# ifftshift of an 8192 x 8192 matrix: which rows each DMA engine takes, and in which steps

## The chip, the core and the metric

The kernel runs on one NeuronCore of a Trainium2 chip (trn2). The time is device microseconds of one execution; of several runs the median is given. No compute engine takes part in the work: the kernel is 256 DMAs from one tensor in the chip's main memory (HBM) to another. A DMA is issued by an instruction on the queue of the SyncE engine (SP) and is carried out by the core's 16 DMA engines, which share it between them.

## The reference

```
def setup_inputs():
    return {"x": np.random.randn(8192, 8192).astype(np.float32)}

def reference(x):
    return np.fft.ifftshift(x)
```

With even sizes the shift swaps the matrix's quadrants: `out[r, c] = x[(r + 4096) % 8192, (c + 4096) % 8192]`. Nothing is computed; 268.4 MB are read and 268.4 MB written. A row is 8192 floats, 32 KB; half a row is 16 KB and a quarter of a row, the piece that one packet carries, is 8 KB.

## The kernel before

`C` is the row length, `hr` and `hc` are half the rows and half the columns. The loop at lines 40 to 42 goes down the matrix in blocks of `rows` = 16 x `apart` = 64 output rows. For each block, two DMAs are issued on `nc.sync`, by the helper `both` (line 25, the DMA itself at line 27): the first with `col` 0, the second with `col` = `piece` = 2048, a quarter of the columns. The access pattern of each has three levels: 64 rows, then two pieces half a row apart, then 2048 contiguous elements. So the first DMA of a block carries the first and third quarter of 64 rows, the second DMA the second and fourth. On the input side the rows are shifted by `hr` and the two pieces come in opposite order (step `-hc`), which is the swap of the halves.

Each DMA is 64 x 2 pieces of 8 KB, 1 MB. By the names in the code (`ENGINES`, `apart`) the outermost level of 64 rows is cut into sixteen runs of four, so that engine `e` takes rows `4e` to `4e + 3` of the block: neighbouring engines are four rows, 128 KB, apart. An engine's eight packets in one DMA are row by row, in each row the two pieces 16 KB apart.

The order of the work is the order of issue on SP's queue: the program is a plain list of 256 DMAs, and there is no wait in the source. The framework gives the DMAs eight completion counters in turn, and the issue of a DMA waits for the one that used the same counter before, eight places earlier. The lines that the change touches:

```
    apart = 4
    piece = hc // 2
    rows = ENGINES * apart
    for row in range(0, R, rows):
        for col in (0, piece):
            both(nc.sync, row, col, rows, piece)
```

Of the kernel before, what the change touches and what calls it, by code (L numbers as in the profile page):

```python
# [1 line left out]

# [4 lines left out]


ENGINES = 16  # L10


@with_exitstack
def kernel(
    ctx: ExitStack,
    tc: tile.TileContext,
    x: bass.AP,
    out: bass.AP,
):
    nc = tc.nc  # L20
    R, C = x.shape
    hr = R // 2
    hc = C // 2

    def both(queue, row, col, rows, piece):

        queue.dma_start(
            out=bass.AP(out.tensor, out.offset + row * C + col, [[C, rows], [hc, 2], [1, piece]]),
            in_=bass.AP(
                x.tensor,  # L30
                x.offset + (row + hr) % R * C + hc + col,
                [[C, rows], [-hc, 2], [1, piece]],
            ),
        )


    apart = 4
    piece = hc // 2
    rows = ENGINES * apart
    for row in range(0, R, rows):  # L40
        for col in (0, piece):
            both(nc.sync, row, col, rows, piece)


# [1 line left out]
_INS = ['x']  # L46
_OUTS = [((8192, 8192), 'float32')]


def kernel(**inputs):  # L50
    import numpy as _np
    import concourse.bacc as _bacc
    import concourse.tile as _tile
    from concourse import mybir as _mybir
    from concourse.bass_utils import run_bass_kernel_spmd as _run

    nc = _bacc.Bacc("TRN2", target_bir_lowering=False, num_devices=1)  # L57
    arrays, args = {}, []
    for name in _INS:
        a = _np.ascontiguousarray(inputs[name])  # L60
        if a.dtype.kind in "iu":
            a = a.astype(_np.int64)
        arrays[f"in_{name}_dram"] = a
        args.append(nc.dram_tensor(f"in_{name}_dram", a.shape, _mybir.dt.from_np(a.dtype), kind="ExternalInput").ap())
    for i, (shape, dtype) in enumerate(_OUTS):
        dt = _mybir.dt.from_np(_np.dtype(dtype))
        args.append(nc.dram_tensor(f"out_{i}_dram", shape, dt, kind="ExternalOutput").ap())
    with _tile.TileContext(nc) as tc:
        kernel(tc, *args)
    r = _run(nc, [arrays], core_ids=[0])  # L70
    got = tuple(r.results[0][f"out_{i}_dram"] for i in range(len(_OUTS)))
    return got[0]
```

## Time and profile before

| what | value |
|---|---|
| time, median of 3 runs | 811.06 us (810.79 to 811.39) |
| the profiled execution's own time | 810.44 us |
| its span, first to last instruction | 808.7 us |
| DMAs, size, median time from issue to landing | 256, 1,024 KB, 25.1 us |
| packets on the DMA queue | 36,864 |
| busy share of the 16 DMA engines | 99.3% |
| mean rate, one direction | 332 GB/s |
| read and written together | 664 GB/s over the span |

The page of the profile has a row of 40 equal slices of the span: the tenths in which the DMA engines were busy, and the GB/s that they moved in it. The queue's line gives packets, megabytes and the time that the packets took as a share of sixteen engines' span. A packet is one contiguous piece of data (or the small write that counts a completion). "To landing" is from the issuing instruction to the arrival of the last completion. SPq in the list of waits is SP's queue; a wait for a DMA there holds back the next issue. Line numbers are those of the kernel.

### The profile page before, as it was taken

To read this page: it belongs to the slowest core of one execution; us is meant where nothing else is said; L and a number is where in the kernel's file an instruction comes from. 1 tells how busy PE (TensorE), PEld (TensorE's weight loads), DVE (VectorE), ACT (ScalarE), POOL (GpSimd) and SP (SyncE) were. 2 spreads that over 40 slices of the span, in tenths; PEclk is the share of its full clock that TensorE was granted. 3 is DMA by queue.
4 is the path that set the end of the run, shared out by engine and by line. 5 is a ranking of instruction groups with operands and counts; after the bars stand their busy time and mean duration, and the time that the engine had idled before them with its cause. 6 is when DMAs were issued, how large, how long until landed. Compare 5 with 4: busy or idle time off the path is not lost. (4 is left out here: it accounts for less than half of the span.)

```text
span 808.7 us, 301 instructions
## 1 busy us (share of the span) xinstructions
POOL 0.2 (0%) x4
## 2 busy tenths in 40 slices
POOL 0000000000000000000000000000000000000000
DMA  8999999999999999999999999999999999999998
GB/s 301 331 335 329 336 334 330 335 332 336 332 335 334 336 331 334 339 328 335 331 335 339 334 334 337 331 336 330 336 334 331 339 332 334 333 336 331 337 335 294
DMA packets 36866, 268.47 MB, mean 332 GB/s; under 512 B 4096, under 2 KB 4096, under 8 KB 4096
## 3 DMA queue, kind: packets, MB, share of 16 engines
q1 hardware_dynamic: 36864, 268.45, 99.3%
q14 instruction: 2, 0.02, 0.0%
HBM read 268.44 MB, written 268.44 MB: 664 GB/s over the span
## 5 line engine op out<-in xcount | busy, mean ns | idle before, releaser
L57 POOL MEMSET const-bfloat16-1.0<- 128x1 bf16 x1 | 0.1, 102 | 0.0
L57 POOL MEMSET const-uint8-127<- 128x1 uint8 x1 | 0.1, 102 | 0.0
L57 POOL MEMSET const-float32-1.0<- 128x1 f32 x1 | 0.1, 99 | 0.0
L57 POOL MEMSET const-float32-0.0<- 128x1 f32 x1 | 0.1, 98 | 0.2 <-issue 0.2
## 6 DMA issues: line engine op xcount, KB each, us to landing
out_dram<-in_x_dram SPq DMA_DIRECT2D x256, 1024.0 KB, 25.1
```

What stands on the lines that cost most here:

```text
L57: nc = _bacc.Bacc("TRN2", target_bir_lowering=False, num_devices=1)
```

## The change

The helper `both`, whose DMA carries two pieces of each row, becomes `copy`, which takes the access pattern from its caller and carries one piece of each row. A block is now 16 x `per` = 128 rows, and four DMAs are issued for it, for the quarters in the order 1, 3, 2, 4. The pattern's outermost level is now 16 long with a step of one row, the next is 8 long with a step of 16 rows: engine `e` takes rows `e`, `e + 16`, ..., `e + 112` of the block. Neighbouring engines are one row (32 KB) apart, and an engine goes in steps of 16 rows (512 KB). The queue, the size of a piece (8 KB), the size of a DMA (1 MB) and the number of DMAs (64 blocks x 4 = 256) stay.

```diff
-    def both(queue, row, col, rows, piece):
-
+    def copy(queue, row, col, dims):
         queue.dma_start(
-            out=bass.AP(out.tensor, out.offset + row * C + col, [[C, rows], [hc, 2], [1, piece]]),
-            in_=bass.AP(
-                x.tensor,
-                x.offset + (row + hr) % R * C + hc + col,
-                [[C, rows], [-hc, 2], [1, piece]],
-            ),
+            out=bass.AP(out.tensor, out.offset + row * C + col, dims),
+            in_=bass.AP(x.tensor, x.offset + (row + hr) % R * C + (col + hc) % C, dims),
         )
 
 
-    apart = 4
+    per = 8
     piece = hc // 2
-    rows = ENGINES * apart
+    rows = ENGINES * per
     for row in range(0, R, rows):
-        for col in (0, piece):
-            both(nc.sync, row, col, rows, piece)
+        for col in (0, hc, piece, hc + piece):
+            copy(nc.sync, row, col, [[C, ENGINES], [ENGINES * C, per], [1, piece]])
```

## The prediction

> **What bounds the kernel now.** I read the page from its top, then the groups of the issuing line, the waits of the issuing queue, the stages, and last the records of single packets. The page first: the span, the slices, the queues.
>
> ```profile
> span 808.7 us, 301 instructions
> ...
> DMA  8999999999999999999999999999999999999998
> GB/s 301 331 335 329 336 334 330 335 332 336 332 335 334 336 331 334 339 328 335 331 335 339 334 334 337 331 336 330 336 334 331 339 332 334 333 336 331 337 335 294
> DMA packets 36866, 268.47 MB, mean 332 GB/s; under 512 B 4096, under 2 KB 4096, under 8 KB 4096
> ...
> q1 hardware_dynamic: 36864, 268.45, 99.3%
> ...
> HBM read 268.44 MB, written 268.44 MB: 664 GB/s over the span
> ...
> out_dram<-in_x_dram SPq DMA_DIRECT2D x256, 1024.0 KB, 25.1
> ```
>
> No compute engine does anything that matters, and the chain of waits on the page is empty of data work. What is seen is that the sixteen DMA engines are 99.3% busy from the first slice to the last, so time can only come from how long a packet takes. The packet count tells how the work is cut: 36,864 = 256 DMAs x 16 engines x 9, eight data packets of 8 KB and one small packet (the 4,096 under 512 B) for each engine and DMA. The GB/s row is flat, 328 to 339 between the ramps, with 331 the commonest low slice.
>
> Next the issuing side, in the waits of SP's queue and the group of the line that issues:
>
> ```profile
> SPq L27 <- DMA out_dram<-in_x_dram: 634.0, 248, 3.2
> SPq L68 <- DMA out_dram<-in_x_dram: 24.1, 4, 15.2
> ...
> L27 SPq DMA_DIRECT2D out_dram<-in_x_dram x256: 562/562/682, 0.7 to 783.1; - x128
> ...
> DMA to landing us min/median/max: 6.0/25.1/26.0
> ```
>
> Each issue takes 562 ns, and 248 of 256 are waited for, 634.0 us in all: each DMA but the first eight waits until the one eight places earlier has landed. 25.1 us to landing over 8 is 3.14 us, the pace of one DMA. SP is idle 2.6 us of each 3.2, so issuing is hidden.
>
> Last the stages (us, POOL busy, clock, DMA share, GB/s):
>
> ```profile
> 4.00:20.00 16.00, 0.00 (x0) 1.00 1.00 342
> 20.00:100.00 80.00, 0.00 (x0) 1.00 1.00 333
> ...
> 400.00:500.00 100.00, 0.00 (x0) 1.00 1.00 335
> ...
> 700.00:780.00 80.00, 0.00 (x0) 1.00 1.00 334
> ```
>
> Nothing drifts with the row number: the rate is 333 to 335 in every long stage; only the first 16 us have 342. From the packet records I worked out what one 8 KB packet takes: median 309 ns, mean 391 ns, 60% of them under 315 ns, a tenth at 605 ns or more, fewest 307 ns. So the engine itself has a pace of 309 ns, and the memory, at 664 GB/s of reads and writes, makes two packets in five wait. The excess is 391 - 309 = 82 ns a packet, or 2,048 packets an engine x 82 ns = 168 us of the run. Check: 2,048 x 391 + 256 x 9 ns (the small packet) = 803 us, the span less its ramps. Those 168 us are all that an order of addresses can change from below; from above nothing caps it.
>
> **The change part by part.** The sum stands against the profiled execution, 810.44 us with a span of 808.7; the median of the three runs is 811.06, 0.6 us (0.08%) more, and I forecast against the median. At the steady rate of 333.6 GB/s the data take 268.44 / 0.3336 = 804.7 us; the rest, 811.1 - 804.7 = 6.4 us, is ramp, last landing and what lies around the span.
>
> *What is removed and added in counts: nothing.* Before, 128 blocks of 64 rows x 2 DMAs of 64 x 2 pieces of 8 KB; after, 64 blocks of 128 rows x 4 DMAs of 16 x 8 pieces of 8 KB. Both are 256 DMAs of 1,024 KB, 8 data packets and a small one per engine. Issue: 256 x 562 ns = 144 us of SP's time in both, hidden under the 634 us of waits. Were an issue to cost more for its new shape, it could grow by 2.6 us before anyone is late; if that cover were gone, every further 1 us of issue is 256 us. Between 0 and that, I take 0, from the 562 ns median that also holds for the present three-level pattern. The bound from below is no gain either, since SP's time is not on the path.
>
> *The wait on the eighth DMA before stays.* The kernel asks for no wait of its own; 248 = 256 - 8 waits come from eight completion counters used in turn. Nothing else is queued behind a waiting SP, and no engine waits for data. Cost 0.
>
> *The ends.* The last DMA is issued at 783.1 us and lands 25 us later, because eight are queued ahead. The sixteen engines finish one DMA within 2.0 us of each other (median of the landing records, 3.0 at most). The new order can change the spread at the last DMA between 0 and 3 us, so by at most 3 us either way. I take 0.
>
> *What moves: which addresses are touched together.* This is the whole change. Before, an engine's eight packets are rows 4e to 4e+3, each with its first and third quarter (then, in the next DMA, second and fourth): steps of 16 KB and back-and-on inside 128 KB, the engines 128 KB apart, one DMA in 2 MB of rows. After, an engine's eight packets are rows e, e+16, ... e+112 in one quarter: every step is 512 KB, neighbouring engines 32 KB apart, one DMA in 4 MB of rows. Reads and writes stay 128 MB plus half a row apart in both. The trace of before has no packet with the new steps, so its cost is bounded by rows. From below: the best stage of before, 342 GB/s, gives 268.44 / 0.342 = 784.9 + 6.4 = 791 us; a lower bound than that has no row. From above: I laid all packets over the interval between the completions of two successive DMAs, in sixteenths; the quickest sixteenth has a mean of 370 ns a packet and the slowest 410 ns. All packets at 410 ns: 2,048 x (410 - 391) = +39 us, 850 us. (All at 370 would be 768 us, further than the 342 GB/s stage; I keep the stage.) Between those ends I take a small loss. The reason: an engine's step is now always 512 KB, so it never returns to the neighbourhood it has just left, where before it does at every second packet; against that the neighbouring engines now lie nearer, 32 KB. What was one engine's locality becomes several engines', and the engines are not in step (completions spread over 2 us, some six packets), so I expect part of it to be lost. For size I take the commonest low slice, 331 GB/s: 268.44 / 0.331 = 811.0 + 6.4 = 817.4 us. The lowest slice, 328, would be 818.4 + 6.4 = 824.8 us.
>
> Beside this, a rule of the Trainium skill speaks against the change: "DMA: Bandwidth & Descriptors", section "Latency and other measured facts", gives copies of 16 KiB rows whose pitch is 512 KiB as 207 GB/s a direction against 214 at full rate, and worse for 2 and 4 MiB; applied to the new steps, an estimate of 804.7 x 214 / 207 + 6.4 = 838 us. No trace here shows a 512 KB step, and the rates there are far below the 334 this kernel holds, so I leave the sum at 817.
>
> **Rivals.** *No difference (811 us, 809.5 to 812.7).* For it: counts equal, and both orders give sixteen streams with different addresses, so the memory may be as full either way; the flat GB/s row over all row numbers speaks for a limit that minds the order little. Against it: 82 ns of waiting a packet is a sensitive quantity; a change of it by 2% already moves the run by 3.4 us. It also covers the case that the packets are dealt to the engines otherwise than the code's names say, which the records (no engine numbers that I can read) cannot exclude.
>
> *Faster, about 797 us (791 to 809).* The mechanism: at one moment the sixteen engines now work side by side within 512 KB instead of 2 MB, and a whole DMA touches one quarter only; neighbours in step could share what one of them has opened. For it: the stage 4 to 20 us, when the engines have just started together, runs at 342 GB/s and its first packets at 314 ns; an order that keeps that would give 791, half of it (338 GB/s: 794.2 + 6.4) about 800, between them 797. It decides once the mean packet falls by more than 0.8 ns. Against: being in step is lost within 20 us of before, and nothing in the new order restores it. A page of the Trainium skill bounds the gain, "HBM Reference", section "Specifications (TRN2)": about 716 GB/s per domain, which would be 268.44 x 2 / 0.716 + 6.4 = 756 us as an estimate; the 664 on the page agree with being near it, so the gain can only be small.
>
> *Much slower, about 838 us (830 to 850, with a tail beyond).* Steps at one large power of two make an engine's packets meet on the same part of the memory, and engines that are some packets apart meet there too, since their distance is then again a multiple of 512 KB plus at most 480 KB. For it: a tenth of the packets now already take 605 ns or more, twice the pace, so collisions exist and are dear. Price: half of the way from 331 GB/s to a mean of 410 ns, and somewhat over, 838. Against: before already has engines at multiples of 128 KB and holds 334.
>
> *DMAs in sequence.* If the new pattern were taken for overlapping ones and each waited for the last, the shortest landing, 6.0 us, x 256 would be 1,536 us. Before has two DMAs interleaved by quarters in the same rows and eight still run together; chance 0.01.
>
> **How the numbers follow.** A small loss (812.7 to 830, named 817) 0.34; much slower 0.17 (of it 0.05 above 850); in sequence 0.01; no difference 0.10; faster 0.38 (of it 0.06 below 791). The likeliest single sign is slower, at 0.34 + 0.17 + 0.01 = 0.52, and inside it the small loss, so 817 us. Differences under 0.2% (1.6 us) are about what three runs, 0.07% apart, can tell from nothing. The range reaches over faster and much slower, 791 to 850, and leaves 0.06 + 0.06 = 0.12 out; the slower case by itself has 812.7 to 850. Both signs are close to each other here, and the range says so.
>
> **What would show it.** Right: 36,864 packets, 256 issues of 1,024 KB near 562 ns, about 25.3 us to landing, 248 waits, the DMA row still at 9, GB/s near 331, the fastest packets still at 307 to 309 ns and the mean at 391 + 6.4 us / 2,048 = 394 ns, with more packets over 600 ns. Wrong: a mean under 390 ns and slices above 336 (then nearness of the engines outweighs the steps); slices of very different rates, or a rate that depends on the row number (then some addresses collide and others don't); a DMA row under 9 (then issuing or dependence became the bound, which I put at nothing); landings far more than 3 us apart among the engines of a DMA.

## The result, and the profile after

The changed kernel takes 813.14 us (median of ten runs, 811.82 to 816.28); the kernel before, run ten times as well, 811.04 us (809.79 to 812.02). The ratio, over all these executions, is 1.0034, with a 95% interval of 1.0021 to 1.0047 (the two medians alone give 1.0026): slower, by a little more than this measurement can tell from nothing. The profiled execution of the changed kernel took 812.23 us. It is the second quickest of the ten and 1.8 us above the profiled execution of before, so the trace shows most of the loss, but not what the slower executions look like inside.

The page of the changed kernel (span, slices, packets, queue, rate, issues), to be read against the page of before:

```profile
span 810.4 us, 301 instructions
...
DMA  8999999999999999999999999999999999999998
GB/s 302 330 334 330 334 333 335 330 336 332 334 335 332 334 334 325 332 334 334 330 336 336 334 334 334 327 329 335 332 334 333 326 337 330 336 334 330 336 336 301
DMA packets 36866, 268.47 MB, mean 331 GB/s; under 512 B 4096, under 2 KB 4096, under 8 KB 4096
...
q1 hardware_dynamic: 36864, 268.45, 98.9%
...
HBM read 268.44 MB, written 268.44 MB: 662 GB/s over the span
...
out_dram<-in_x_dram SPq DMA_DIRECT2D x256, 1024.0 KB, 25.2
```

Packets, bytes and DMAs are the same to the last one. Two things differ: the slices now go down to 325, and the queue's packets fill 98.9% of sixteen engines' time instead of 99.3%. In microseconds of one engine, busy is 0.989 x 810.4 = 801.5 against 0.993 x 808.7 = 803.0, and not busy is 8.9 against 5.7. So the packets themselves have become 1.5 us *shorter* in sum, and the time without a packet 3.2 us longer; the difference, 1.7 us, is that of the two spans. The packet records say the same: a mean of 390.1 ns an 8 KB packet, 391.0 before.

The group of the line that issues, and the waits of SP's queue, of the changed kernel:

```profile
L26 SPq DMA_DIRECT2D out_dram<-in_x_dram x256: 571/571/690, 0.7 to 785.2; - x128
...
DMA to landing us min/median/max: 6.1/25.2/26.0
```

```profile
SPq L26 <- DMA out_dram<-in_x_dram: 634.2, 248, 3.3
SPq L63 <- DMA out_dram<-in_x_dram: 23.7, 4, 14.9
```

An issue takes 571 ns instead of 562, and SP still waits 634 us in 248 waits: issuing is as hidden as it was. The stages (us, POOL busy, clock, DMA share, GB/s) of the changed kernel are flat too, the first again the quickest:

```profile
4.00:20.00 16.00, 0.00 (x0) 1.00 1.01 345
20.00:100.00 80.00, 0.00 (x0) 1.00 0.99 332
...
400.00:500.00 100.00, 0.00 (x0) 1.00 1.00 334
...
700.00:780.00 80.00, 0.00 (x0) 1.00 1.00 334
```

For the experiments I worked out three more quantities from the packet records of each profiled execution, over its steady part (from about 19 us after its start to 40 us before its end). The first is the mean time of a packet, the second the share of time at which 13 or fewer packets were under way. (The records carry no engine numbers; with sixteen engines, 13 packets mean that at least three engines have none.) This share is 0.04% before and 1.5% after. In the changed kernel two thirds of this time lie in some 25 stretches of 200 to 540 ns, mostly with 13 packets under way and in a few with 9 to 12; the kernel before has practically none. The third, the mean busy share, sums the packet times over sixteen engines' time; packets of one engine overlap a little, so it is good to a few tenths of a per cent. Below, "moments" are these times, and "the share of time with 13 or fewer engines" is this quantity.

### The profile page after: what moved, and what is told of

It reads as the page before. It is cut to its first block, busy times and chain, and to the rows that moved or that the text cites. A ratio compares the mean times of both kernels' runs of the same rounds, so it can differ in the third digit from the quotient of the medians.

```text
span 810.4 us, 301 instructions
## 1 busy us (share of the span) xinstructions
POOL 0.2 (0%) x4
## 3 DMA queue, kind: packets, MB, share of 16 engines
q1 hardware_dynamic: 36864, 268.45, 98.9%
HBM read 268.44 MB, written 268.44 MB: 662 GB/s over the span
## 6 DMA issues: line engine op xcount, KB each, us to landing
out_dram<-in_x_dram SPq DMA_DIRECT2D x256, 1024.0 KB, 25.2
```

## The experiments

Theories to begin with: A, the prediction's (an engine's steps of 512 KB make packets wait longer); G (the gaps come at the ends of DMAs and are paid per DMA); S (the longer issue). Each ratio is to the kernel before, run on the same chip beside it, with its 95% interval.

**The changed kernel again.** No edit.

> The changed kernel once more, beside the others of this group. Its trace had packets of 390.1 ns on average against 391.0 before, so not slower ones, but 0.23 of an engine idle on average in the steady part against 0.14 before, mostly just behind the completion writes. Theory G (gaps at the ends of DMAs): ratio 1.002 to 1.005, packet mean again at or under that of before, idle share again larger. Theory A (the 512 KB steps make packets slower, the prediction's): the mean packet is at least 1.3 ns above that of before in a second trace. If the ratio's interval reaches 1.000 the whole difference is in doubt.

Measured: 1.0033 (1.0021 to 1.0046), on a chip where the kernel before takes 822.66 us instead of 811. Time without packets is there again (1.7% of the time with 13 or fewer engines). The loss is real and small. The mean packet, 396.3 ns, belongs to this slower chip, on which no trace of before was taken, so it does not speak on A.

**Consecutive rows for an engine.**

```diff
-            copy(nc.sync, row, col, [[C, ENGINES], [ENGINES * C, per], [1, piece]])
+            copy(nc.sync, row, col, [[per * C, ENGINES], [C, per], [1, piece]])
```

> As after, but engine e takes 8 consecutive rows (8e to 8e+7): engines 256 KB apart, steps of 32 KB; quarters, order, size and number of DMAs as after. It undoes the steps of 16 rows and the 1-row spacing alone. Theory A: time returns to that of before, 811 us, ratio 0.998 to 1.002. Theory G, if the gaps come from one quarter per DMA: stays at 813 to 814 with the larger idle share; if they come from the engines lying 1 row apart: 811 and the idle share of before, 0.14. Issue theory S (571 ns for an issue instead of 562, 256 x 9 ns = 2.3 us): 813, since the issue has the same three levels as after.

Measured: 1.0036 (1.0018 to 1.0053), 1.6% of the time with 13 or fewer engines. Steps of 32 KB instead of 512 KB, engines 256 KB apart instead of 32: the same time. So the loss is there without the 512 KB steps, which speaks against A; strictly, the distance between engines changed along with the step, and a gain from one could hide a loss from the other. The row pairs below have no 512 KB step at the engine distance of before. This DMA also takes only 511 ns to issue, less than the 562 of before, and is no quicker for it: S falls too.

**The quarters in the order 1, 2, 3, 4.**

```diff
-        for col in (0, hc, piece, hc + piece):
+        for col in (0, piece, hc, hc + piece):
```

> As after, but the quarters in the order 1, 2, 3, 4: successive DMAs of a block lie 8 KB apart, reads too. All theories that put the loss into the steps or the ends of DMAs: same as after, 813, within 0.2%. If the order 1, 3, 2, 4 is what keeps successive DMAs on different parts of the memory: slower, 820 or more, with more packets over 600 ns.

Measured: 1.0043 (1.0029 to 1.0057), an interval that overlaps that of the changed kernel's repeat (1.0021 to 1.0046). The order costs at most a little.

**Twice the rows in a DMA, half as many DMAs.**

```diff
-    per = 8
+    per = 16
```

> As after, but 256 rows and 2 MB in a DMA: 128 DMAs, 16 packets an engine, steps of 512 KB as after. Half as many ends of DMAs and half as many issues. Theory G: the extra idle halves, time falls by about half of the 2.8 us, 811.5 to 812.5, idle share about 0.18 or less. Theory A: the steps are unchanged, so 813 to 814 and the packet mean as after. Theory S: half of 2.3 us gone, 812.

Measured: 1.0044 (1.0029 to 1.0058). Half the ends and half the issues take nothing off. G falls in the form that the cost is paid per DMA. (An issue of these 2 MB DMAs takes 6.0 us in the median, and no waits between them are listed: what held back the next issue as a wait now sits in the issue itself. The same holds for the 2 MB DMAs of the kernel before, below, so the two can be compared.) What these four have in common is one quarter of the columns in a DMA; that became theory Q.

**The kernel before, for a second trace.** No edit.

> The kernel before, for a trace on the chip of this group. All theories: packet mean about as the changed kernel's on the same chip; if the idle share is a property of the kernel and not of one execution, the engines' busy share in the steady part is again above 0.998 (0.9992 in the first trace), where the four kernels with one quarter per DMA had 0.993 to 0.996.

Measured: 811.36 us; in the packet records of the steady part the engines' mean busy share is 0.9995 (0.9992 in the first trace), mean packet 391.7 ns, no moment with 13 or fewer engines busy. So the absence of such moments belongs to the kernel and not to one execution.

**The kernel before with 128 rows in a DMA.**

```diff
-    apart = 4
+    apart = 8
```

> The kernel before with 128 rows instead of 64 in a DMA: both halves of each row still in one DMA, engines 8 rows apart, 128 DMAs of 2 MB, 16 packets an engine. Theory Q (the loss is from one quarter per DMA, that is from all engines reading one half of the columns and writing the other for a whole DMA): 1.000, within 0.2%, busy share above 0.998. Theory R (the loss is from more rows, 128 or 256, per DMA): 1.003 to 1.005, as with the 256-row kernel of one quarter.

Measured: 1.0012 (1.0002 to 1.0021), no moments. Beside 1.0044 for the 2 MB DMAs of one quarter this is for Q.

**Both halves, rows 16 apart.**

```diff
-            out=bass.AP(out.tensor, out.offset + row * C + col, [[C, rows], [hc, 2], [1, piece]]),
+            out=bass.AP(out.tensor, out.offset + row * C + col, [[ENGINES * C, rows], [hc, 2], [1, piece]]),
...
-                [[C, rows], [-hc, 2], [1, piece]],
+                [[ENGINES * C, rows], [-hc, 2], [1, piece]],
...
-    for row in range(0, R, rows):
-        for col in (0, piece):
-            both(nc.sync, row, col, rows, piece)
+    for block in range(0, R, rows * ENGINES):
+        for row in range(block, block + ENGINES):
+            for col in (0, piece):
+                both(nc.sync, row, col, rows, piece)
```

> The kernel before with rows 16 apart in a DMA: both halves of a row in a DMA as before, but an engine's next row is 512 KB on (the step of the changed kernel) and the engines are 2 MB apart. Theory A (the 512 KB steps cost, the prediction's): 1.003 or slower. Theory Q: 1.000, within 0.2%. Much slower, 1.02 or more, if engines 2 MB apart meet on the same part of the memory.

Measured: 1.0576 (1.0558 to 1.0595). Here packets did get longer, 415.2 ns in the steady part. The page of this kernel:

```profile
DMA  9999999999999999999999999999999999999999
GB/s 284 316 316 317 315 314 317 317 318 314 311 315 314 316 311 313 316 315 313 316 314 316 314 314 315 317 319 318 313 317 313 312 316 317 313 322 310 317 317 284
...
HBM read 268.44 MB, written 268.44 MB: 627 GB/s over the span
```

Between the ramps every slice is at 310 to 322 with the engines as busy as ever: the rate is lower everywhere. Steps and distance between engines (2 MB) changed together here; later runs tell more.

**One quarter, rows in pairs, the pattern's shape as written in the kernel before.**

```diff
-    per = 8
+    apart = 4
...
+    rows = ENGINES * apart
+    far = R // 4
+    for half in (0, hr):
+        for row in range(half, half + far, rows):
+            for col in (0, hc, piece, hc + piece):
+                copy(nc.sync, row, col, [[C, rows], [far * C, 2], [1, piece]])
```

> The access pattern of before in shape (64 rows, two pieces, 2048 contiguous; engines 4 rows apart), but the two pieces are the same quarter of rows r and r + 2048 instead of two quarters of one row; quarters in the order 1, 3, 2, 4 as after. One quarter per DMA with the issue shape and engine split of before. Theory Q: 1.003 to 1.004 and busy share 0.993 to 0.996. If the loss comes from the shape of the pattern or its cost at issue (16 x 8 against 64 x 2): 1.000.

Measured: 1.0032 (1.0014 to 1.0049), 1.4% of the time with 13 or fewer engines: as Q says. But its executions scatter, 810.71 to 819.10 us, and the profiled one is the quickest, 810.71 us. Its page:

```profile
span 808.9 us, 301 instructions
...
q1 hardware_dynamic: 36864, 268.45, 98.9%
...
HBM read 268.44 MB, written 268.44 MB: 664 GB/s over the span
```

This is the rate of before (664 GB/s) with the unfilled time of after (98.9%): packets of 389.7 ns make up for it. It is one execution, the quickest of twelve, and a first sign that the moments with idle engines are not what the time is lost in.

**Two quarters from row pairs**, once two halves (first and third, second and fourth), once neighbours (first and second, third and fourth). In the row-pair kernel the second piece moves to another column:

```diff
-                copy(nc.sync, row, col, [[C, rows], [far * C, 2], [1, piece]])
...
+                        [[C, rows], [far * C + second - col, 2], [1, piece]],
```

with `second = (col + hc) % C` in the one, and the neighbouring quarter in the other; the input side follows in the same way.

> As the row-pair kernel (64 rows, two pieces an engine 2048 rows apart), but the second piece comes from the quarter half a row further: first and third, then second and fourth quarter in one DMA, from rows r and r + 2048. Theory Q (what costs is that a DMA stays in one quarter, so that all engines read one half of the row and write the other): back to 0.999 to 1.002, moments with 13 or fewer engines busy under 0.2% of the time, against 1.4% of the pair in one quarter. Rival P (what helps before is that the two pieces are of one row, 16 KB apart): 1.003, and 1.4% again.

> As the row-pair kernel, but the second piece comes from the neighbouring quarter of the same half (first and second, third and fourth), rows r and r + 2048. If the mixing of the halves (16 KB) matters: 1.003 and moments with 13 or fewer engines busy above 1%, as with one quarter. If any two quarters in one DMA do: 1.000 and under 0.2%.

Measured: 1.054 (1.051 to 1.057) and 1.051 (1.049 to 1.053), and neither answers the question. The six executions of the first scatter from 851.79 to 892.67 us; its ratio is that of the two quickest, and the profiled one took 870.04 us. Issue and waits of this execution:

```profile
out_dram<-in_x_dram SPq DMA_DIRECT2D x256, 1024.0 KB, 8.6
```

```profile
SPq L42 <- DMA out_dram<-in_x_dram: 692.3, 128, 10.6
```

A DMA lands 8.6 us after its issue instead of 25.1, and there are 128 waits of up to 10.6 us instead of 248 of up to 3.2: the queue is run nearly dry again and again. In the trace the third and the fourth DMA of each block wait for the first and the second. Presumably the framework took these patterns, whose pieces lie in different columns, for overlapping ones; that it put other waits in is seen, why is not. The engines' packets fill 89.5% of the time. What can be read from it: with fewer DMAs in flight a packet is quicker (377.8 ns in the steady part), and the time is lost all the same to engines without a packet.

**Engines 2 MB apart, steps of 32 KB.**

```diff
-    rows = ENGINES * per
-    for row in range(0, R, rows):
-        for col in (0, hc, piece, hc + piece):
-            copy(nc.sync, row, col, [[C, ENGINES], [ENGINES * C, per], [1, piece]])
+    rows = 64
+    for block in range(0, R, ENGINES * rows):
+        for row in range(block, block + rows, per):
+            for col in (0, hc, piece, hc + piece):
+                copy(nc.sync, row, col, [[rows * C, ENGINES], [C, per], [1, piece]])
```

> One quarter per DMA, each engine 8 consecutive rows (steps of 32 KB), engines 64 rows = 2 MB apart. The kernel with rows 16 apart was 1.058; it had 512 KB steps and engines 2 MB apart together. If the distance of the engines made that: 1.05 to 1.065 here, packets of 410 ns or more. If the 512 KB steps made it: 1.003 to 1.005, as with engines 256 KB apart.

Measured: 1080 to 1190 us, the quickest execution 1080.05 / 810.97 = 1.33 times the time of before; no interval is given, since the executions scatter so much. The page of the profiled one, the longest at 1189.96 us:

```profile
q1 hardware_dynamic: 36864, 268.45, 98.7%
...
HBM read 268.44 MB, written 268.44 MB: 452 GB/s over the span
```

The engines are as full as after the change, and a packet takes 572 ns. So it is the distance between engines that hurts, not an engine's own step: with 512 KB steps and the same 2 MB (1.058) the loss was far smaller than with 32 KB steps, although there both halves were in a DMA and here one quarter is.

**Packets of 16 KB.**

```diff
-    apart = 4
-    piece = hc // 2
+    apart = 2
+    piece = hc
...
-        for col in (0, piece):
+        for col in (0,):
```

> The kernel before with packets of 16 KB: 32 rows, both whole halves of each row in one DMA of 1 MB, engines 2 rows apart, four data packets an engine. Theory Q: halves are mixed in every DMA, so no lost moments (under 0.2%) and 0.997 to 1.002; it is faster only if some of the 82 ns of waiting a packet is paid per packet and not per byte.

Measured: 1.0030 (1.0018 to 1.0041), 0.03% of the time with 13 or fewer engines. Halves are mixed, the moments are absent, and the time is lost nevertheless. A packet takes 785.8 ns, 2 x 392.9: half as many packets save none of the waiting.

**Both halves of every second row.**

```diff
-            out=bass.AP(out.tensor, out.offset + row * C + col, [[C, rows], [hc, 2], [1, piece]]),
+            out=bass.AP(out.tensor, out.offset + row * C + col, [[2 * C, rows], [hc, 2], [1, piece]]),
...
-                [[C, rows], [-hc, 2], [1, piece]],
+                [[2 * C, rows], [-hc, 2], [1, piece]],
...
-    for row in range(0, R, rows):
-        for col in (0, piece):
-            both(nc.sync, row, col, rows, piece)
+    for block in range(0, R, rows * 2):
+        for row in (block, block + 1):
+            for col in (0, piece):
+                both(nc.sync, row, col, rows, piece)
```

> The kernel before with every second row in a DMA: both halves of 64 rows, 2 rows apart, so engines 256 KB apart and steps of 64 KB, as far apart as in the kernel of one quarter and 8 consecutive rows (1.0036). Its pattern has two levels on both sides (64 x 2), as the changed kernel's has (16 x 8). Theory Q (one quarter per DMA costs): 0.999 to 1.002, 13 or fewer engines busy in under 0.2% of the time. If the two levels or the 256 KB were the cause: 1.003 and above 1%.

Measured: 1.0033 (1.0019 to 1.0048), and 0.04% of the time with 13 or fewer engines. Of Q's expectation the moments came true and the time did not: mixing the halves does away with the moments, and the time stays lost. Q falls as the cause of the time, and the moments, as counted here, with it; they are a mark of one quarter per DMA at these distances. But this kernel is not free of unfilled time:

```profile
q1 hardware_dynamic: 36864, 268.45, 99.1%
```

In the steady part the engines' mean busy share is 0.996, against 0.9992 before and 0.994 after, only spread too thin to count as moments, and the missing 0.3% is about its whole loss. That the loss needs no unfilled time is shown by the 16 KB packets: busy share above 0.999, packets longer (392.9 ns for 8 KB, against 391.3 and 391.7 in the two traces of before), 1.0030.

**Columns not swapped.**

```diff
-            in_=bass.AP(x.tensor, x.offset + (row + hr) % R * C + (col + hc) % C, dims),
+            in_=bass.AP(x.tensor, x.offset + (row + hr) % R * C + col, dims),
```

> The changed kernel without the swap of the column halves (the rows are still shifted, the columns are copied straight, so that part of the computation is left out): all engines read and write the same quarter. If what costs is that all read one half of the row and write the other: 1.000 and moments under 0.2%. If it is one quarter in a DMA as such: 1.003 and moments above 1%, as in the changed kernel. If reading and writing the same quarter collide: slower than 1.005, with longer packets.

Measured: 1.0061 (1.0036 to 1.0086), 1.8% of the time with 13 or fewer engines. Doing away with the crossing of the halves takes away neither the loss nor the moments.

**Two queues.**

```diff
-        for col in (0, hc, piece, hc + piece):
-            copy(nc.sync, row, col, [[C, ENGINES], [ENGINES * C, per], [1, piece]])
+        for k, col in enumerate((0, hc, piece, hc + piece)):
+            copy((nc.sync, nc.scalar)[k % 2], row, col, [[C, ENGINES], [ENGINES * C, per], [1, piece]])
```

> The changed kernel with its DMAs dealt to two queues, first and second quarters on SP, third and fourth on ACT, so that each engine has packets of two halves at once. Theory Q, in the form that an engine must mix halves from packet to packet: 0.999 to 1.002, few idle moments. If only the make-up of a single DMA counts: 1.003. If two queues cost by themselves, slower than 1.005.

Measured: 1.0046 (1.0034 to 1.0059), 1.3% of the time with 13 or fewer engines. (Dealt in the order 1, 3, 2, 4, SP has the first and second quarters and ACT the third and fourth.) Nothing is gained by offering each engine two DMAs.

**Engines 512 KB apart, steps of 32 KB.**

```diff
-    rows = ENGINES * per
-    for row in range(0, R, rows):
-        for col in (0, hc, piece, hc + piece):
-            copy(nc.sync, row, col, [[C, ENGINES], [ENGINES * C, per], [1, piece]])
+    rows = 16
+    for block in range(0, R, ENGINES * rows):
+        for row in range(block, block + rows, per):
+            for col in (0, hc, piece, hc + piece):
+                copy(nc.sync, row, col, [[rows * C, ENGINES], [C, per], [1, piece]])
```

> One quarter per DMA, each engine 8 consecutive rows, engines 16 rows = 512 KB apart. With 32 KB apart (after) 1.0034, with 256 KB 1.0036, with 2 MB 1.33 or more. If the loss at 2 MB grows with the distance from the start: 1.05 to 1.15 here. If there is a sharp limit above 512 KB: 1.003 to 1.006.

Measured: 1.0534 (1.0514 to 1.0553). The page of this kernel:

```profile
GB/s 289 318 313 319 313 320 321 314 321 316 319 317 320 315 315 317 320 313 319 308 319 315 314 317 319 316 320 309 318 316 315 316 316 318 318 318 317 321 314 293
...
q1 hardware_dynamic: 36864, 268.45, 99.5%
...
HBM read 268.44 MB, written 268.44 MB: 631 GB/s over the span
```

The engines are full (99.5%) and every slice is low; a packet takes 412.6 ns in the steady part. Between 256 KB (1.0036) and 512 KB the loss goes from a third of a per cent to five.

**512 KB in a DMA, in both forms.** The kernel before with `apart = 2`, and the changed kernel with `per = 4`:

```diff
-    apart = 4
+    apart = 2
```

```diff
-    per = 8
+    per = 4
```

> The kernel before with 32 rows in a DMA: 512 DMAs of 512 KB, consecutive rows, both halves, packets 16 KB apart, engines 64 KB apart. Theory V (consecutive rows together with both halves keep the rate): 0.998 to 1.0015 and at least 0.2% better than the 64-row kernel of one quarter beside it. Rival D (the 1 MB and the 128 KB between engines are a narrow best point, and any other form loses): 1.003 or more. It also tells whether smaller DMAs beat both kernels (below 0.998).

> The changed kernel with 64 rows in a DMA: 512 DMAs of 512 KB, one quarter each, rows 1 apart between engines and 16 in an engine. Theory V: 1.003 to 1.005, as with 128 rows (1.0034) and 256 rows (1.0044). Rival D: 1.003 or more too, and no better or worse than the 32-row kernel of both halves. If the prediction's sum over 512 KB steps were right after all, fewer steps a DMA would not change it: 1.003.

Measured: 1.0021 (1.0012 to 1.0030) and 1.0027 (1.0017 to 1.0038). The two are the same within their intervals, so theory V (consecutive rows with both halves keep the rate) is not borne out at this size either. The smaller DMAs also have twice the small packets that count completions: 256 more an engine at 9 ns each are 2.3 us, 0.28%, about the whole loss of the first of them, so the pair says little on the addresses. No form that was run beats the kernel before.

The forms with the whole computation and engines at most 256 KB apart whose DMAs were not held back, in one list (ratio; mean packet in the steady part, which on the slower chip, marked *, is longer for all; share of time with 13 or fewer engines busy):

| kernel | engines apart | step in an engine | ratio | packet ns | moments |
|---|---|---|---|---|---|
| before | 128 KB | 16 KB | 1 | 391.3 | 0.04% |
| both halves, 128 rows | 256 KB | 16 KB | 1.0012 | 394.2 | 0.00% |
| both halves, 32 rows | 64 KB | 16 KB | 1.0021 | 391.3 | 0.10% |
| both halves, 16 KB packets | 64 KB | 16 KB | 1.0030 | 785.8 for 16 KB | 0.03% |
| both halves, every second row | 256 KB | 16 and 48 KB | 1.0033 | 392.4 | 0.04% |
| after | 32 KB | 512 KB | 1.0034 | 390.4 | 1.5% |
| after, two queues | 32 KB | 512 KB | 1.0046 | 391.9 | 1.3% |
| one quarter, 64 rows | 32 KB | 512 KB | 1.0027 | 391.9 | 1.7% |
| one quarter, row pairs | 128 KB | to the pair, 64 MB | 1.0032 | 389.7 | 1.4% |
| one quarter, order 1234 * | 32 KB | 512 KB | 1.0043 | 395.7 | 1.3% |
| one quarter, 256 rows * | 32 KB | 512 KB | 1.0044 | 398.2 | 1.4% |
| one quarter, 8 rows * | 256 KB | 32 KB | 1.0036 | 397.1 | 1.6% |

## Why the prediction was right or wrong

*What bounds the kernel* held. The sixteen engines stay filled (98.9%), and what takes time is packets longer than the quickest (390.1 ns in the mean, 307 at the least); where a run was much slower, either the packets were longer with full engines (engines 512 KB and 2 MB apart) or, in the two kernels held back, the engines were not filled.

*Counts, issue, waits, ends: right at nothing.* 256 DMAs, 36,864 packets, 248 waits, 25.2 us to landing. The issue grew by 9 ns, hidden as said; the kernel with the shortest issue, 511 ns, shows that it would not matter the other way either. One remark there was wrong: the present pattern is not a three-level one as issued. Since half a row's step and the row's step are one to two, 64 x 2 pieces at one distance become a single level of 128 on the output side (so the trace lists the issue), and 562 ns was the price of that.

*What moves: the sign was right, the mechanism and the size were wrong, so the right sign is luck.* The step that failed is "an engine's step is now always 512 KB, so it never returns to the neighbourhood it has just left ... I expect part of it to be lost", sized at 331 GB/s, 817.4 us. The text had promised that packets would wait longer, 394 ns in the mean; in the trace it is 390.1, 391.0 before, and the time lost in that execution is time without a packet (8.9 us an engine, 5.7 before). Nor are the 512 KB steps needed for the loss: with steps of 32 KB and engines 256 KB apart it is 1.0036, with row pairs at the engine distance of before 1.0032, after the change 1.0034. The distance between engines, which I weighed on the other side as a help, is what costs, but only at the 512 KB (1.053) and 2 MB that were tried, and no more at 256 KB (1.0036) than at 32 KB (1.0034); the change moved it from 128 to 32 KB, inside the flat part. In the terms of the sum: the measured 813.1 us less the 6.4 us of ramp is 268.44 / 806.7 = 332.8 GB/s, where 331 was taken and 333.6 stands for no change. The +6 us of the forecast were +2.1 us by the medians, and 2.8 us by the ratio.

*What the loss of a third of a per cent is made of stays open.* Runs exclude, each as the one cause of all these losses: the 512 KB steps, the order of the quarters, the number of DMAs, the cost of an issue, the levels of the pattern, and the idle moments; and without the crossing of the halves the loss is no smaller (1.0061). The idle moments are the tempting story, since they are in every kernel of one quarter a DMA at small distances; but kernels without them lose as much (every second row, 1.0033; 16 KB packets, 1.0030), and one execution full of them runs as fast as before (row pairs, 810.71 us). That several small causes meet, another one in each kernel, is not excluded: the time is lost as unfilled time in some and as longer packets in others. Part of the loss is also scatter: with engines 256 KB apart and steps of 32 KB the executions lie between 822.11 and 829.37 us, those of the kernel before beside them between 821.21 and 823.91. What is left is a description: the kernel before sits at the best of a flat stretch, and eleven other forms beside it lie 0.1 to 0.5% higher.

*The rivals.* "No difference" ended at 812.7 us, just under the result; its reason, that sixteen different streams fill the memory either way, comes nearest to what the runs show. "Faster" fell: neighbours 32 KB apart share nothing that shows, and the first stage alone is quick (345 GB/s, 342 before). "Much slower" did not come with the change, but a loss of its size exists where the engines, and not one engine's packets, are at a large distance; that addresses then meet on the same part of the memory is not shown. "DMAs in sequence", put at 0.01, did not come either; a milder form of it, each second pair waiting for the pair before, came in one of my own kernels, and other waits in a second.

*The rule on pitches.* The Trainium skill, "DMA: Bandwidth & Descriptors", section "Latency and other measured facts", has copies getting slower with the row pitch, 207 GB/s at 512 KiB and 164 at 2 MiB against 214. The runs agree with such a loss for the distance between engines (1.053 at 512 KB, 1.33 and more at 2 MB), and for an engine's own step of 512 KB they show none of that size (1.0034). I had applied the rule to the step, which gave the 838 us that I left out of the sum.

## What to carry to other kernels

Where DMA engines are 99% filled and the memory moves some 660 GB/s, count first what is the same: if bytes, packets and waits are, an order of addresses was worth a few tenths of a per cent here so long as the engines stayed within 256 KB of their neighbours. Look at the distance between engines working at the same moment before looking at one engine's steps: 512 KB cost five per cent here, and 2 MB from six per cent to a third and more. All the distances tried are powers of two, so the runs do not tell a large distance as such from one that is a multiple of a large power of two; engines 17 rows (544 KB) apart would, and were not run. And a mark in the trace that goes with the slower kernel (engines idle at once) is a cause only if the time moves with it; one kernel that loses the mark and keeps the time shows that it is not the only one.

## What the runs showed that I had not expected

- At 2 MB between engines, larger steps within an engine went with the smaller loss: 1.058 with 512 KB steps and both halves, 1.33 or more with 32 KB steps and one quarter. Which of the two differences does it was not separated.
- Time without packets and time in packets can trade against each other: an execution with 98.9% filled engines ran at the same 664 GB/s as one with 99.3%. The filled share by itself says nothing of the rate here.
- The time of an issue follows the pattern's levels: 511 ns (128 pieces in one level on both sides), 562 (one level on the output side), 571 to 573 (two levels), in DMAs of up to 1 MB whose waits are listed apart; with 2 MB DMAs the issue itself is held back, to 5.9 and 6.0 us in the median.
- Chips differ more than the kernels do: the kernel before takes 822.66 us on one chip and 810.6 to 811.4 on the others, with the same ratio of after to before, 1.0033 and 1.0034.
